# The second half's forget, query, gate and pool projections as 2x2x2 block products, in a streaming encoder trunk

## The chip, the core and the metric

The kernel runs on one core of a Trainium2 chip. The metric is the device time of one launch in microseconds (us). Six names are used below. PE is TensorE, the matrix engine, and its weight loads have a row of their own in the profile (PEld). DVE is VectorE, ACT is ScalarE, POOL is GpSimd, and SP is the engine whose queue issues nearly all transfers. Each engine runs its instructions in the order in which they stand in its own program, and waits on semaphores for the others.

## The reference, cut to what matters

One layer is applied to 2048 prompt tokens and to 32 tokens of a running stream (the sample). The width is 1024, everything is float32.

```
h = rmsnorm(x, g_pre_mix)
u, zq, zf, zi, zg = split(h @ w_in, ...)              # five times 512 columns
y_pool = window means of u (2, 4, 8, 16 frames) - u, then a 128x128 map per group
q = silu(zq);  fgate = lb + (1-lb)*sigmoid(zf);  kin = (1-lb)*sigmoid(-zf)
o, S1 = HGRN2 recurrence(q, kin, v = zi, log fgate)    # 4 heads of 128, state 128x128
y_hg = rmsnorm(o) * silu(zg)
x = x + rmsnorm(concat(y_pool, y_hg) @ w_out, g_post_mix)
h2 = rmsnorm(x, g_pre_ffn)
x = x + rmsnorm((silu(h2 @ w_gate) * (h2 @ w_up)) @ w_down, g_post_ffn)
```

The last 15 rows of u and the final states of the recurrence are outputs too, for the prompt and for the sample.

## The kernel before

**Precision.** A float32 operand is split into a high part, rounded by a cast on ACT, and a low part, the difference, made on DVE. A product of two such operands is three matmuls into one PSUM bank: high by high, high by low, low by high. All large products are matmuls of a 128x128 weight tile with 128x512 activations.

**Stages.** The prompt is cut in two halves of 1024 tokens, A and B, and the sample rides with B. A half runs through: values (the zi columns, lines of `values`), the front (16 column tiles of 128: forget, query and gate of four heads in `head_products`, then four tiles of u in `pool_products`), the projection by w_out (`project`), and gate and up (`gate_up`). The product by w_down is run for both halves at the end (`down`). In the trace the second half's values take 797 to 843 us, its front 843 to 1086 us, and its projection begins at 1086 us.

**Two ways of multiplying.** In the front a column tile is 8 row blocks of the weights by 2 blocks of 512 tokens by 3 matmuls, which is 48 matmuls into the banks `mmb`. In gate and up two column tiles of weights and the two blocks of tokens and of rows are taken as a 2x2x2 block product that needs seven block products where the plain way needs eight (a Strassen form). Its sums of activation blocks are made once per half (`first_forms`, `last_forms`), its sums of weight blocks for each pair of columns. A product is 12 matmuls into one of the banks `gx`, `gz`, `gy`, and four results `c11`, `c21`, `c22`, `c12` are put together from them by ACT (a copy of a bank) and DVE (an addition of a bank).

**What sets the order.** PE's order is written out: tasks (the recurrence of a head, the window sums, the loads of the next stage) are generators that are polled after every third matmul and that give the PE time until their next step. The other engines are ordered by the tile scheduler, which also gives out buffer slots. SP has one queue in order. Every matmul is recorded under the helper at line 202. Other lines that are spoken of: 1325 is the low part of a weight form in gate and up, 1427 the addition that empties the bank `gy` into `c22`, 1250 the low part of the hidden activations, 724 the copies of the values out of PSUM, 240 and 246 the low parts of weights, 858 a step of the recurrence on POOL (`k_t`), 929 its small copies (`attn`), and 1531 to 1547 the sums for the product by w_down, the only large two-input additions that POOL does here. `hst` and `hd` are the hidden activations on their way through DRAM, 256 KB a transfer.

## Time and profile before

| | |
|---|---|
| time, median of 3 runs | 2083.34 us (2080.56 to 2084.01) |
| span of the profiled execution | 2079.3 us |
| granted TensorE clock | 0.999 |
| PE busy | 2068.0 us, 99% of the span |
| DVE, ACT, POOL busy | 1418.5, 834.6 and 279.7 us |
| data moved | 319.49 MB |

The profiled execution has no time of its own beside its span; the median is 4.0 us longer than that span, and this difference is taken as what lies around a span. Busy times of PE are modelled, so its rate is read from stretches of the chain in which one kind of matmul follows another: a row "start, duration, what, xN" there gives the time per matmul.

### The profile page before, as it was taken

What the parts mean: (1) busy time and instruction counts of PE and PEld (TensorE: products, weight loads), DVE (VectorE), ACT (ScalarE), POOL (GpSimd) and SP (SyncE); (2) the same over time, 40 slices, a digit from 0 to 9 for tenths busy, and PEclk for the clock granted to TensorE, in tenths of its full rate; (3) what the DMA queues carried; (4) which work ended last, traced back from release to release, by engine and by line L of the source; (5) the groups of instructions that cost most, each with busy time, mean ns of one, the idle gap of its engine ahead of it and who ended that gap; (6) DMA issues with size and microseconds to landing.
All of it is one profiled execution on the core that took longest, in us unless ns stands there. A gap on an engine that the chain in (4) does not pass through costs nothing.

```text
span 2079.3 us, 34073 instructions
## 1 busy us (share of the span) xinstructions
PE 2068.0 (99%) x13093; PEld 1686.5 (81%) x13093; DVE 1418.5 (68%) x2288; ACT 834.6 (40%) x1656; POOL 279.7 (13%) x375
## 2 busy tenths in 40 slices
PE   9999999999999999999999999999999999999998
PEld 7788888888888888788888788888888778888876
DVE  5655665787777778465575697776666866566587
ACT  6444445654444445233334563444444521011032
POOL 0232302100000000122231200000000210110134
PEclk9999999999999999999999999999999999999999
DMA  8321144445555558211015614554445796776778
GB/s 288 115 88 42 44 142 162 132 127 167 161 153 152 157 172 260 70 46 36 26 54 177 200 52 137 163 149 139 147 137 173 231 335 203 218 226 200 219 223 220
DMA packets 391777, 319.49 MB, mean 154 GB/s; under 512 B 18216, under 2 KB 320800, under 8 KB 391616
## 3 DMA queue, kind: packets, MB, share of 16 engines
q1 hardware_dynamic: 389168, 309.41, 48.1%
q0 software_dynamic: 2016, 7.34, 1.9%
q8 instruction: 103, 1.69, 0.3%
q10 hardware_dynamic: 432, 0.57, 0.1%
q14 instruction: 58, 0.48, 0.1%
HBM read 216.79 MB, written 100.47 MB: 153 GB/s over the span
## 4 chain that ended last, share of the span: by engine, by line
PE 96%; DVE 2%; DMA 1%; ACT 0%; issue 0%; POOL 0%; DVEq 0%; SPq 0%; ACTq 0%; POOLq 0%
PE gx L202 23%; PE mmb L202 16%; PE gy L202 12%; PE dx L202 10%; PE ops L202 10%; PE gz L202 5%; PE dy L202 5%; PE vps L202 4%; PE dz L202 3%; PE gb L202 1%; PE gw L202 1%; PE gsps L202 1%; PE ups L202 1%; DVE acc L1605 1%; PE tps L345 1%; PE fps L202 1%
## 5 line engine op out<-in xcount | busy, mean ns | idle before, releaser
L202 PE MATMUL gx<-fhi,wf 128*128 128x512 f32 x1376 | 386.9, 391 | 0.0
L202 PEld LDWEIGHTS gx<-fhi,wf 128*128 128x128 f32 x1376 | 256.8, 188 | 54.9 <-issue 2.2
L202 PE MATMUL gx<-flo,wf 128*128 128x512 f32 x688 | 213.1, 390 | 0.0
L202 PE MATMUL gy<-fhi,wf 128*128 128x512 f32 x704 | 201.6, 390 | 0.0
L202 PE MATMUL dx<-dhi,hst 128*128 128x512 f32 x640 | 185.4, 391 | 0.8 <-DVE acc L1605 0.7
L202 PE MATMUL mmb<-hTlo,whi 128*128 128x512 f32 x512 | 175.3, 404 | 0.0
L202 PE MATMUL mmb<-hThi,whi 128*128 128x512 f32 x512 | 165.5, 404 | 0.0
L1605 DVE TENSOR_TENSOR acc<-dx,acc 128x512 f32<-128x512 f32 x168 | 115.1, 690 | 71.6 <-PE dx L202 70.6
L202 PE MATMUL mmb<-hThi,wlo 128*128 128x512 f32 x512 | 158.8, 391 | 0.0
L1325 DVE TENSOR_TENSOR wf<-s,wf 128x512 fp32r<-128x512 f32 x176 | 120.2, 690 | 56.0 <-ACT wf L1320 54.0
L202 PEld LDWEIGHTS gy<-fhi,wf 128*128 128x128 f32 x704 | 131.8, 188 | 28.1 <-DVE c L1427 0.4
L202 PEld LDWEIGHTS gx<-flo,wf 128*128 128x128 f32 x688 | 129.1, 188 | 27.0
L1320 ACT CAST wf<-s 128x512 fp32r<-128x512 f32 x176 | 108.1, 623 | 102.8 <-DVE s L1301 31.5
L202 PEld LDWEIGHTS dx<-dhi,hst 128*128 128x128 f32 x640 | 119.5, 188 | 30.1 <-issue 3.4
L1544 ACT CAST dhi<-t 128x1024 fp32r<-128x1024 f32 x20 | 20.7, 1055 | 249.8 <-DVE dlo L1545 181.6
L1325 DVE TENSOR_TENSOR wf<-wraw,wf 128x512 fp32r<-128x512 f32 x132 | 89.8, 687 | 34.4 <-ACT wf L1320 34.4
L202 PEld LDWEIGHTS mmb<-hTlo,whi 128*128 128x128 f32 x512 | 96.2, 188 | 20.5 <-issue 0.8
L202 PEld LDWEIGHTS mmb<-hThi,wlo 128*128 128x128 f32 x512 | 96.3, 188 | 18.9 <-issue 0.2
L1320 ACT CAST wf<-wraw 128x512 fp32r<-128x512 f32 x132 | 80.8, 622 | 75.8 <-PE gx L202 36.2
L202 PE MATMUL gy<-flo,wf 128*128 128x512 f32 x352 | 108.7, 389 | 0.0
L202 PEld LDWEIGHTS mmb<-hThi,whi 128*128 128x128 f32 x512 | 91.8, 188 | 20.6 <-issue 3.3
L202 PE MATMUL dx<-dlo,hst 128*128 128x512 f32 x320 | 98.6, 389 | 0.0
(326 smaller groups left out, 3974.8 us busy)
## 6 DMA issues: line engine op xcount, KB each, us to landing
hst<-hdFalse SPq DMA_DIRECT2D x140, 256.0 KB, 2.9
hst<-hdTrue SPq DMA_DIRECT2D x140, 256.0 KB, 3.0
wraw<-in_w_gate_dram SPq DMA_DIRECT2D x50, 512.0 KB, 4.0
wraw<-in_w_up_dram SPq DMA_DIRECT2D x50, 512.0 KB, 3.9
hdFalse<-hhi SPq DMA_DIRECT2D x77, 256.0 KB, 2.3
hdFalse<-hlo SPq DMA_DIRECT2D x77, 256.0 KB, 2.2
hdTrue<-hhi SPq DMA_DIRECT2D x77, 256.0 KB, 2.2
hdTrue<-hlo SPq DMA_DIRECT2D x77, 256.0 KB, 2.5
```

The source lines that it names most:

```text
L202: nc.tensor.matmul(out, l, r, start=start, stop=stop, skip_group_check=more)
L345: nc.tensor.transpose(ps[:, c:c + P], xn[:, (2 * kp + kk) * P:(2 * kp + kk + 1) * P], ident)
L1320: nc.scalar.copy(wf[:, 0], getattr(M, src) if isinstance(src, str) else src)
L1325: nc.vector.tensor_tensor(wf[:, 1], getattr(M, src) if isinstance(src, str) else src, wf[:, 0].bitcast(F32), ALU.subtract)
L1544: nc.scalar.copy(hi, src)
L1605: nc.vector.tensor_tensor(dst, ps, dst, ALU.add)
```

## The change

Only the second half's front is changed in what PE multiplies; the rest follows from it.

- **Products.** The 16 column tiles of half B are taken as 8 pairs (forget with query of a head, gate with gate of two heads, u with u of two groups). A pair is seven products of 12 matmuls, in the order 1, 2, 6, 7, 5, 4, 3, in `front_pairs`.
- **Weight forms.** They lie ready in DRAM (`wd`). Three of the seven are plain blocks, and half A's front writes their high and low parts out when it has them (`keep`, 48 writes of 256 KB). The other four are sums: a task in half A's gate and up (`weight_forms`) loads 32 blocks, makes 32 sums of 128x512 on POOL, 32 casts on ACT, 32 differences on DVE, and writes 64 tiles. Half B's front loads 112 tiles of 256 KB, three products ahead. From the second pair on, and within the first, each load stands behind a copy of one element on POOL, which reads a result tile of the product round and so marks the time from which the load may be issued.
- **Activation forms.** The normalised channels of half B are kept as four blocks. Three forms are plain blocks, which the values use too. The other four need two pairs of sums on DVE and two pairs on POOL (128x1024 each), 8 casts and 8 differences of 128x1024.
- **Space.** To hold the forms, values go to DRAM (`vd`) and come back for each head, the results of heads 0 to 2 go to `yd` and come back before the projection, the slots shrink to 1024 columns, and one pool of tiles grows from 21 to 25.
- **Sample.** Its loads and statistics move to the start of the program and its column tiles into half A's front, where the weights pass by anyway. Its recurrence is done for the four heads at once in a task of half B (`sample_mix`), instead of 32 extra columns in each head.
- **Recurrence and windows.** A head's recurrence is split in two tasks (its tail may run beside the next head), and the window sums take the frames before the half from small tiles. The projection of half B takes its row blocks in another order.

```diff
...
-NT = 21
+NT = 25
...
+FETCH = 3
+FORMS = 8000.0
 LOOKRAW = 2
-TMAX = HALF + NS
-SLOT = HALF + 64
+SLOT = HALF
...
-        KORDER = [4, 5, 2, 3, 0, 1, 6, 7]
+        KORDER = [[4, 5, 2, 3, 0, 1, 6, 7], [4, 5, 2, 3, 6, 7, 0, 1]]
+        COLS = (COL_F, COL_Q, COL_G, 0)
+        FQ, G, U = (lambda h: ((0, h), (1, h))), (lambda h: ((2, h), (2, h + 1))), (lambda g: ((3, g), (3, g - 1)))
+        PAIRS = [FQ(0), G(0), FQ(1), FQ(2), G(2), FQ(3), U(3), U(1)]
+        ROUND = (1, 2, 6, 7, 5, 4, 3)
+        wd = [DP.tile([7, P, 2, 512], F32, name=f"wd{i}") for i in range(len(PAIRS))]
+        vd = DP.tile([NH, P, NCH, P], F32, name="vd")
+        yd = DP.tile([NH - 1, 2, P, HALF], F32, name="yd")
...
+        def keep(w, kind, h):
+            n, m = pair_of(kind, h)
+            for p, kh in ((4, 1),) if m else ((1, 0), (2, 1)):
+                for i in range(2):
+                    nc.sync.dma_start(out=wd[n][p - 1, :, i, :], in_=w[1 + i][kh].bitcast(F32))
...
+        def weight_block(n, m, kh):
+            kind, h = PAIRS[n][m]
+            c0 = COLS[kind] + h * P
+            t = t2("wb", [P, 4, P])
+            nc.sync.dma_start(out=t, in_=w_in[kh * 512:kh * 512 + 512, c0:c0 + P].rearrange("(k p) c -> p k c", p=P))
+            return t.rearrange("p k c -> p (k c)")
...
+        def weight_forms():
+            def put(n, p, src):
+                hi, lo = t2("fhi", dt=F32R), t2("flo", dt=F32R)
+                nc.scalar.copy(hi, src)
+                nc.vector.tensor_tensor(lo, src, hi.bitcast(F32), ALU.subtract)
+                for i, t in enumerate((hi, lo)):
+                    nc.sync.dma_start(out=wd[n][p - 1, :, i, :], in_=t.bitcast(F32))
...
+            v = nc.gpsimd
+            for n in range(len(PAIRS)):
+                a21, a22 = weight_block(n, 1, 0), weight_block(n, 1, 1)
+                yield FORMS
+                v.tensor_tensor(a22, a21, a22, ALU.add)
+                a11 = weight_block(n, 0, 0)
+                yield FORMS
+                put(n, 5, a22)
+                v.tensor_tensor(a21, a11, a21, ALU.subtract)
+                v.tensor_tensor(a11, a22, a11, ALU.subtract)
+                a12 = weight_block(n, 0, 1)
+                yield FORMS
+                put(n, 7, a21)
+                v.tensor_tensor(a12, a12, a11, ALU.subtract)
+                yield FORMS
+                put(n, 6, a11)
+                yield FORMS
+                put(n, 3, a12)
...
+                    if tg == 0:
+                        nc.scalar.copy(hi[:, parts[i]], flat[:, parts[i]])
+                if tg:
+                    nc.scalar.copy(hi, flat)
+                for cs in parts:
+                    nc.vector.tensor_tensor(lo[:, cs], flat[:, cs], hi[:, cs].bitcast(F32), ALU.subtract)
...
+            b11, b21 = S.xT[0][0:2], S.xT[0][2:4]
+            b12, b22 = S.xT[1][0:2] if tg else None, S.xT[1][2:4] if tg else None
+            F = S.plain[tg]
+            if tg == 0:
+                S.F[1], S.F[2] = F[0:2], F[2:4]
+                return
+            S.F[3] = F[2:4]
+            v = nc.vector
+            yield 5000.0
+            sums(b12, b12, b11, ALU.subtract)
+            t2s = [ztile("t2s", [P, D]) for _ in range(2)]
+            sums(t2s, b22, b12, ALU.subtract)
+            yield 3000.0
+            S.F[6] = form(t2s)
+            sums(b11, t2s, b11, ALU.subtract, nc.gpsimd)
+            yield 3000.0
+            sums(b21, b21, t2s, ALU.subtract, nc.gpsimd)
+            S.F[7] = form(b11)
+            yield 3000.0
+            S.F[5] = form(b12)
+            yield 3000.0
+            S.F[4] = form(b21)
...
+            if not S.B:
+                for h in range(NH):
+                    for c in (COL_F, COL_Q, COL_G):
+                        want(lambda c=c, h=h: raw_cols(w_in, c + h * P))
+                for g in (3, 2, 1, 0):
+                    want(lambda g=g: raw_cols(w_in, g * P))
+                project_loads(S)
...
+                vt = t2("vt", [P, NH, P])
+                (nc.vector.tensor_copy if i % 2 else nc.scalar.copy)(vt, pss[i].rearrange("p (h c) -> p h c", c=P))
+                nc.sync.dma_start(out=vd[:, :, tg * 4 + i, :].rearrange("h p c -> p h c"), in_=vt)
...
+            def fetch(i, behind=None):
+                if i < len(seq):
+                    n, p = seq[i]
+                    wf[n, p] = [t2("wf", dt=F32R) for _ in range(2)]
+                    for j, t in enumerate(wf[n, p]):
+                        if behind is not None:
+                            nc.gpsimd.tensor_copy(t[0:1, 0:1], behind[0:1, 0:1])
+                        nc.sync.dma_start(out=t.bitcast(F32), in_=wd[n][p - 1, :, j, :])
+            def product(i, ps, start, behind):
+                n, p = seq[i]
+                fetch(i + FETCH, behind)
+                while p not in S.F:
+                    S.norm[1].step()
+                hi, lo = wf.pop((n, p))
+                for k in (0, 2):
+                    trios = [(hi[:, kk * P:(kk + 1) * P], lo[:, kk * P:(kk + 1) * P],
+                              *(x[:, (kk % 2) * 512:(kk % 2) * 512 + 512] for x in S.F[p][kk // 2])) for kk in (k, k + 1)]
+                    for m, (a, b) in enumerate(in_turn(trios)):
+                        mm(ps, a, b, start and k == 0 and m == 0, k == 2 and m == 5, rcost(512), not start)
+                        if m % 3 == 2:
+                            poll()
+            for i in range(FETCH):
...
+            c21 = None
+            add = ALU.add
+            for n, pair in enumerate(PAIRS):
+                i = n * len(ROUND)
+                for kh in pair:
+                    targets(S, *kh)
+                x = mmbank("gx")
+                product(i, x, True, c21)
+                c11 = t2("c11")
+                nc.scalar.copy(c11, x)
+                z = mmbank("gz")
+                product(i + 1, z, True, c21)
+                nc.vector.tensor_tensor(c11, z, c11, add)
+                use(S, *pair[0], c11, 0, 512)
+                product(i + 2, x, False, c11)
+                c21 = t2("c21")
+                nc.scalar.copy(c21, x)
+                y = mmbank("gy")
+                product(i + 3, y, True, c11)
+                c22 = t2("c22")
+                nc.scalar.copy(c22, y)
+                product(i + 4, x, False, c21)
+                nc.vector.tensor_tensor(c22, x, c22, add)
+                use(S, *pair[1], c22, 512, 1024)
+                if n + 1 == len(PAIRS):
+                    project_loads(S)
+                    ahead(Stream.used)
+                product(i + 5, y, False, c22)
+                nc.vector.tensor_tensor(c21, y, c21, add)
+                use(S, *pair[1], c21, 0, 512)
+                product(i + 6, x, False, c22)
+                use(S, *pair[0], x, 512, 1024)
+                if pair[0][0] == 0:
+                    S.hgrn = start_head(S, pair[0][1], 3500.0)
+                elif pair[0][0] == 3:
+                    for _, g in pair:
+                        S.pools[g] = S.pool = Task(pool_window(S, g, S.e[g]), 1500.0, after=S.pool)
+            S.hgrn.finish()
+            for h in range(NH - 1):
+                S.y[4 + h] = (ztile("yhi", dt=F32R), ztile("ylo", dt=F32R))
+                for i, t in enumerate(S.y[4 + h]):
+                    nc.sync.dma_start(out=t.bitcast(F32), in_=yd[h, i])
...
             yield 1200.0
+            if B:
+                S.tails = Task(hgrn_tail(S, H, h, spill, kds, vs, qa, t7), 0.0, after=S.tails)
+            else:
+                yield from hgrn_tail(S, H, h, spill, kds, vs, qa, t7)
...
+                while not hasattr(H, "g"):
+                    yield 2000.0
+                nc.vector.tensor_tensor(yr, yps, H.g[:, cols], ALU.mult)
+                if spill:
+                    for i, t in enumerate(two(yr)):
+                        nc.sync.dma_start(out=yd[h, i, :, cols], in_=t.bitcast(F32))
+                else:
+                    put_y(S, 4 + h, cols, yr)
...
+                    pairs = front_pairs(S)
+                    next(pairs)
...
+                if i:
+                    next(pairs, None)
+                else:
+                    for h in range(NH):
+                        head_products(S, h)
+                    for g in (3, 2, 1, 0):
+                        pool_products(S, g)
...
+                if i == 0:
+                    forms = Task(weight_forms(), 50000.0)
...```

The order of instructions shows the change at three places. First PE at the start of half B's front. Its rows before, where `hThi` and `hTlo` are the parts of the activations and `whi` and `wlo` those of the weights:

```order
L202 MATMUL vsps<-wrow,hsr 32x512 x4
L202 MATMUL mmb<-hThi_7402,whi 128x512
L202 MATMUL mmb<-hThi_7404,whi 128x512
L202 MATMUL mmb<-hTlo_7403,whi 128x512
L202 MATMUL mmb<-hTlo_7405,whi 128x512
L202 MATMUL mmb<-hThi_7402,wlo 128x512
L202 MATMUL mmb<-hThi_7404,wlo 128x512
```

and now, with `fhi`, `flo` the parts of an activation form and `wf` those of a weight form:

```order
L203 MATMUL vsps<-wrow,hsr 32x512 x4
L203 MATMUL gx<-fhi,wf 128x512 x2
L203 MATMUL gx<-flo,wf 128x512 x2
L203 MATMUL gx<-fhi,wf 128x512 x4
L203 MATMUL gx<-flo,wf 128x512 x2
L203 MATMUL gx<-fhi,wf 128x512 x2
L203 MATMUL gz<-fhi,wf 128x512 x2
L203 MATMUL gz<-flo,wf 128x512 x2
L203 MATMUL gz<-fhi,wf 128x512 x4
L203 MATMUL gz<-flo,wf 128x512 x2
L203 MATMUL gz<-fhi,wf 128x512 x2
L203 MATMUL gx<-fhi,wf 128x512 x2
```

A product is 12 matmuls, and the bank changes with it. In the whole program the matmuls on `mmb` go from 1536 to 768, and those on `gx`, `gz` and `gy` grow by 384, 96 and 192.

Second, DVE from the middle to the end of half B's values. Before, only low parts (`hlo` of half A's hidden activations, `wlo`) and sums for them stood between the last parts of the activations and the last copies out of the values' banks:

```order
L1250 TENSOR_TENSOR hlo<-c_7510,hhi 128x512
L246 TENSOR_TENSOR wlo<-wraw,whi 128x512 x2
L1250 TENSOR_TENSOR hlo<-hs,hhi 128x512
L1250 TENSOR_TENSOR hlo<-c_7360,hhi 128x512
L1243 TENSOR_TENSOR hs<-c_7360,hs 128x512
L724 COPY va<-vps 128x512
L724 COPY vb<-vps 128x512
```

Now (`xT` are the activation blocks, summed in place, `t2s` a sum, `flo` a form's low part, `vt` the values):

```order
L370 TENSOR_TENSOR xT<-xT 128x1024
L810 COPY vt<-vps 128x512
L370 TENSOR_TENSOR xT<-xT 128x1024
L370 TENSOR_TENSOR t2s<-xT 128x1024 x2
L365 TENSOR_TENSOR flo<-t2s,fhi 128x1024
L1500 TENSOR_TENSOR hs<-c_7884,c_8190 128x512
L365 TENSOR_TENSOR flo<-t2s,fhi 128x1024
L241 TENSOR_TENSOR wlw<-wrow,whw 128x1024
L1510 TENSOR_TENSOR hlo<-hs,hhi 128x512
L365 TENSOR_TENSOR flo<-xT,fhi 128x1024 x4
L1510 TENSOR_TENSOR hlo<-c_8087,hhi 128x512
L365 TENSOR_TENSOR flo<-xT,fhi 128x1024 x2
```

The four sums and eight differences of the forms now stand ahead of the last two copies of values that DVE does. POOL's four sums are released by the sums on `t2s`.

Third, POOL in the second and third pair, where a head's recurrence runs:

```order
L1018 TENSOR_TENSOR k_t<-k_t,tt 128x16x32
L920 CAST wf<-c_8956 1x1 x2
L1226 COPY attn_8818<-cmp 32x4x32 x4
L1226 COPY attn_8819<-cmp 32x4x32 x3
L1018 TENSOR_TENSOR k_t<-k_t,tt 128x8x64
L1226 COPY attn_8819<-cmp 32x4x32
L920 CAST wf<-c_9278 1x1 x4
L920 CAST wf<-c_9368 1x1 x2
```

The `CAST` rows are the markers, one for each of the two parts of a weight form. They are new on this engine, and stand among the steps of the recurrence that were there before.

599 lines of the change are left out of this document (337 added, 262 removed).

## The prediction

> **What bounds the kernel now.** I read the page first, for the engine that is full, then the windows of half B's front and of the stages around it, then the chain for the time of one matmul.
>
> ```profile
> span 2079.3 us, 34073 instructions
> PE 2068.0 (99%) x13093; PEld 1686.5 (81%) x13093; DVE 1418.5 (68%) x2288; ACT 834.6 (40%) x1656; POOL 279.7 (13%) x375
> PE 96%; DVE 2%; DMA 1%; ACT 0%; issue 0%; POOL 0%; DVEq 0%; SPq 0%; ACTq 0%; POOLq 0%
> L202 PE MATMUL mmb<-hTlo,whi 128*128 128x512 f32 x512 | 175.3, 404 | 0.0
> hst<-hdFalse SPq DMA_DIRECT2D x140, 256.0 KB, 2.9
> ```
>
> PE is 99% of the span and 96% of the chain. No idle time stands before the matmuls of the front (last column 0.0), so a matmul taken out of it shortens the chain by its own time, as long as nothing else takes its place.
>
> Columns of the windows: length, then busy us (instructions) of PE, PEld, DVE, ACT, POOL, the granted clock, the DMA share, GB/s.
>
> ```profile
> 450.00:800.00 350.00, 350.00 (x1545) 289.64 (x1544) 263.22 (x416) 163.20 (x287) 3.38 (x7) 1.00 0.56 166
> 842.00:1086.00 244.00, 244.00 (x2846) 198.72 (x2839) 148.18 (x329) 81.86 (x236) 67.00 (x93) 1.00 0.15 44
> 1620.00:2000.00 380.00, 379.82 (x1704) 304.24 (x1703) 238.47 (x322) 63.70 (x90) 49.58 (x21) 1.00 0.76 233
> ```
>
> The second row is the front that changes: PE 244.00 of 244, DVE 61%, ACT 34%, POOL 27%, DMA 0.15. There is room on every other engine. The first row is half A's gate and up, where the weight forms are to be made: DVE is at 263 of 350 there, POOL all but free.
>
> The group means (404 ns) are the latency of a pipelined matmul. The rate is in the chain:
>
> ```profile
> 791.65 5.44 PE gx L202 x24
> 797.09 32.64 PE vps L202 x144
> 841.83 0.99 PE vsps L202 x8
> 842.83 7.71 PE mmb L202 x33
> 902.74 1.85 PE ups L202 x16
> ```
>
> 32.64 us for 144 and 5.44 for 24 are both 226.7 ns per 128x512 matmul, whichever bank it writes. The front begins at 842.83; I call the corresponding moment T0.
>
> **The change, term by term, against the span of 2079.3 us.**
>
> *Matmuls.* Removed: 768 x 0.2267 = 174.1 us. Added: 56 products x 12 = 672 x 0.2267 = 152.3 us (2.72 us a product). Net −21.8 us. Accumulating into a bank round by round doesn't change the rate: the `gx` row above is such a product.
>
> *Sample.* Its column tiles move from one full stage of PE into another: nothing. Batching its recurrence removes 12 fp32 matmuls of 128x128, two records each, at 0.116 us a record (1.85 / 16): −2.8 us. It adds five of that kind (+1.2) and one four times as wide (4 x 0.23, +0.9), and drops three transposes of one record each (−0.3). Net −1.0; bounds −2 and 0.
>
> *First pair, activation forms.* DVE before, around the end of the values:
>
> ```profile
> 802.12 1.41 DVE L493 SCALAR_TENSOR_TENSOR xT<-xT,cons,rb 128x512 f32<-128x512 f32 x2 [4.17 <-DMA rb<-roots]
> 822.40 1.23 DVE L240 TENSOR_TENSOR wlw<-wrow,whw 128x1024 fp32r<-128x1024 f32 x1
> 823.54 0.69 DVE L1250 TENSOR_TENSOR hlo<-hs,hhi 128x512 fp32r<-128x512 f32 x1
> 828.45 0.69 DVE L1243 TENSOR_TENSOR hs<-c,hs 128x512 f32<-128x512 f32 x1
> 839.15 0.69 DVE L724 COPY va<-vps 128x512 f32<-128x512 f32 x1 [10.01 <-PE vps L202]
> ```
>
> DVE is solid from 802.12 to 829.14 and then has 10.01 us free. A 128x1024 operation takes 1.14 us of its queue (822.40 to 823.54), a 128x512 one 0.6. After the change DVE has between the same points 8 scalings (5.6 us by the first row), 12 differences, 5 weight parts and 4 sums of 128x1024 (21 x 1.14 = 23.9), and 7 operations of 0.6 (4.2): 33.7 us, to 835.8. What makes this dearer is POOL, which makes four of the sums in that time. How the two engines get on stands at the end of gate and up, the one place where POOL does such sums now:
>
> ```profile
> 1609.38 0.69 DVE L1240 TENSOR_TENSOR hs<-c,c 128x512 f32<-128x512 f32 x1
> 1611.31 1.62 POOL L1532 TENSOR_TENSOR t<-wdr,t 128x512 f32<-128x512 f32 x1
> 1611.70 1.78 DVE L1545 TENSOR_TENSOR dhl<-wdr,dhl 128x512 fp32r<-128x512 f32 x1
> 1612.89 1.74 POOL L1533 TENSOR_TENSOR t<-wdr 128x512 f32<-128x512 f32 x1
> 1613.62 1.56 DVE L1545 TENSOR_TENSOR dhl<-t,dhl 128x512 fp32r<-128x512 f32 x1
> L1531 POOL TENSOR_TENSOR t<-wdr 128x1024 f32<-128x1024 f32 x5 | 12.0, 2400 | 108.6 <-DMA wdr<-in_w_down_dram 82.3 <-DVE acc L1605 17.8 <-PE gx L202 8.5
> ```
>
> A DVE operation that takes 0.69 us alone took 1.78 and 1.56, and ended 0.55 us after the POOL sum that ran beside it; so while POOL sums, DVE does one operation per sum. Four sums of 2.4 us are 9.6 us in which DVE does 4 x 1.14: 5.0 us lost, to 840.8. The copy of values that PE's second product needs stands behind all of it and must be done by T0 + 2.7 = 845.5. Cover of about 4 us; without it, up to 5 us if sums and casts serialise.
>
> [...]
>
> *First pair, weights.* The loads of the fourth product stand in SP's queue behind the last four writes of values, which wait for copies after the values' last matmul. An issue takes 0.49 us and a load lands 2.9 us later:
>
> ```profile
> 1655.59 3.42 SPq L1558 DMA_DIRECT2D hst<-hdTrue  x7
> ```
>
> Copies to T0 + 1.5, six issues (2.9), landing (2.9): T0 + 7.3, needed at T0 + 8.2. Both parts of the first pair together: 0 to 6, and I take 2, nearer the covered end, since both sums come out in time but by 1 to 4 us.
>
> *Later pairs.* A load is issued three products ahead, 8.2 us. Behind its marker stand: the drain of the bank on DVE (0.69), the copy on POOL, the issues (1.0 for two), the landing (2.9): 4.9 us with an idle POOL (0.33 for the copy, an eighth of the row of copies below), so 3.3 us to spare. Bandwidth is no limit: 512 KB per 2.72 us is 193 GB/s at most, and 233 GB/s were moved in the third window beside PE at 379.82 of 380. But the markers stand in POOL's queue behind a head's recurrence:
>
> ```profile
> 952.98 1.50 POOL L858 TENSOR_TENSOR k_t<-k_t,tt 128x512 f32<-128x512 f32 x1 [2.25 <-issue]
> 954.50 2.62 POOL L929 COPY attn<-cmp 32x128 f32<-32x128 f32 x8
> ```
>
> A step and the eight copies are 4.1 us, 0.8 more than there is to spare, once per head: 3 us if a marker meets it each time. Behind a marker that waits stand the recurrence's next steps on POOL, and PE's small matmuls that use them are late in turn. The same steps hold DVE, as above. Bounds 0 and 10 (four heads, two such meetings of 1.2 us each); I take 2.
>
> *Transfers without a price.* The 48 writes of half A's front, the values' way through DRAM and the reloads of `yd` fall into stages where the DMA share is 0.15 to 0.56; if one is late, it is a wait of one landing, 2.9 us, at one place, and lies within the bounds above.
>
> *Gate and up of half A.* 32 sums on POOL, 32 differences on DVE (22 us of the 87 that are free there), 32 casts on ACT; the traffic grows by 25 MB in some 320 us, 166 to 245 GB/s, near what the third window carried. PE feels DVE at one place per 19 us round, where `gy` is emptied:
>
> ```profile
> 506.71 0.69 DVE L1427 TENSOR_TENSOR c<-gy,c 128x512 f32<-128x512 f32 x1
> 508.61 0.62 PE L202 MATMUL gy<-fhi,wf 128*128 128x512 f32 x2
> ```
>
> The bank is free at 507.40 and written again at 508.61: 1.2 us to spare. A sum of 128x512 on POOL (1.62) holds a DVE operation up by 1.1, just inside; the two sums that stand together hold two, and are outside by 1.0. Eight such groups: 0 to 8, and I take 1, since a group meets the drain in few of the 19 us.
>
> *Start of the projection.* The last pair is u, and its window sums end on DVE. After the last product DVE has, in its order, 18 operations of 0.6, 7 of 1.14 to 1.2 and three small ones: 19 us to the last low part. PE reads it after some 76 matmuls, 17.2 us. And the first weight part stands behind the last head's output, late by 0.6. I take 2.5; bounds 1 (reads partly covered by the order of row blocks) and 5 (as above with POOL's share).
>
> The sum: 2079.3 − 21.8 − 1.0 + 2 + 2 + 1 + 2.5 = 2064.0 for the span, 15.3 us less. The median of the runs is 4.0 above the span, so 2068 us.
>
> **Rivals.**
>
> *All of it stays* (the covers hold everywhere): 2083.3 − 21.8 − 1.0 = 2060.5. For it: the covers above are there on paper. Against it: two of them are under 1.5 us.
>
> *The weight stream is late in every round.* Before, nothing of the front's weights waited for a result; now each fetch runs through DVE, POOL and SP. It decides when drain, marker and landing exceed 8.2 us, that is a landing over 6.2 or a POOL queue over 3.3 us. 0.3 us on each of 56 products is 17 us and leaves 2083.3 − 22.8 + 17 + 5.5 = 2083; 0.7 us makes 2105. For it: SP's queue is in order and holds writes that wait. Against it: landing is 2.9 at 233 GB/s.
>
> *POOL's sums hold DVE, and DVE holds PE in gate and up*, on the other side: eight rounds have a single sum, a pair and a single sum. If each meets a drain with DVE's queue full, a single costs 1.62 − 1.2 = 0.4 and a pair 3.2 − 1.2 = 2.0, 2.8 a group, 22 in all: 2083.3 − 22.8 + 22 + 6.5 = 2089, slower. It decides from 2 us a group on. For it: the 1.78 us above. Against it: the groups are spread over 320 us and forms of weights can wait. [...]
>
> *It doesn't do what it says*: the order of instructions has the 96 matmuls less, so only a slower rate would do it, about 2083.
>
> **How the numbers follow.** Chances: the sum, with 2062 to 2076 as its own range, 0.66; all stays 0.10; weights late 0.12 (0.06 of it faster, 0.03 within, 0.03 slower); POOL and DVE 0.10 (0.01, 0.01, 0.08); no effect 0.02. The predicted time is 2068. The range runs from 2059 (sample at its better bound) to 2085 (every product a little over 0.3 us late). What this measurement tells from no change is about 0.2%, 4.2 us. Faster by more: 0.66 + 0.10 + 0.06 + 0.01 = 0.83; within: 0.03 + 0.01 + 0.02 = 0.06; slower: 0.03 + 0.08 = 0.11.
>
> **What would show it.** The stretch from the values' last matmul to the projection's first should be about 244 − 22 = 222 us, with PE idle of 1 to 4 us in its first 12 us and in the first 20 of the projection. Idle before `gx`, `gy`, `gz` put down to a transfer of `wf` is the late stream; idle before `gy` put down to DVE between 450 and 800 us is the third rival. If gate and up of half A is longer than before by over 3 us, my price there is wrong; if the front is shorter by less than 15 us, that of the later pairs is.

## The result and the profile after

The change is not faster but a little slower: 2088.32 us, median of 5 runs (2085.35 to 2091.79), against 2081.29 us for the kernel before in 5 runs beside it (2080.56 to 2084.01). The ratio is 1.0029, with a 95% interval of 1.0017 to 1.0041. The prediction was 2068. The profiled execution of the kernel after is the fastest of its five (2085.35 us), so its stages below come to some 3 us less than the median; where those 3 us lie no trace shows. Time and span of one execution lie 1.7 to 1.9 us apart in all runs, not the 4.0 taken ahead of the prediction, so the forecast span of 2064.0 stands for 2066 rather than 2068, which changes nothing in what follows.

The page of the kernel after, its head, the totals of the engines and the shares of the chain of waits:

```profile
span 2083.6 us, 34762 instructions
PE 2054.5 (99%) x12980; PEld 1667.7 (80%) x12980; DVE 1476.4 (71%) x2320; ACT 850.1 (41%) x1663; POOL 378.9 (18%) x544
PE 82%; DVE 9%; DMA 3%; issue 2%; ACT 2%; POOL 1%; SPq 0%; DVEq 0%; ACTq 0%; POOLq 0%
```

PE did less: 12980 records against 13093, and 13.5 us less busy time. But the span is 4.3 us longer, and PE's share of the chain fell from 96% to 82%: other engines, DVE first, now set the end in places.

The stages, from the first matmul of each on PE to the first of the next (in the last stage to PE's end), in us, from one profiled execution of each version. The last three columns are versions that are told of below: weight sums on DVE, activation sums on DVE, and the last version.

| stage | before | after | weight sums on DVE | activation sums on DVE | last version |
|---|---|---|---|---|---|
| front A | 233.8 | 254.5 | 254.7 | 253.0 | 249.5 |
| projection A | 90.7 | 91.0 | 91.0 | 91.0 | 91.0 |
| gate and up A | 422.7 | 429.9 | 423.6 | 430.2 | 424.5 |
| values B | 45.8 | 47.0 | 46.2 | 45.8 | 45.8 |
| front B | 243.7 | 215.9 | 215.7 | 212.5 | 209.5 |
| projection B | 97.5 | 100.0 | 102.1 | 99.1 | 101.1 |
| gate and up B | 452.4 | 453.6 | 453.2 | 453.4 | 453.3 |
| down | 434.9 | 434.5 | 434.3 | 434.5 | 434.8 |

Where the time went is read from this table first. By the prediction's terms the products and the batched recurrence save 22.8 us in front B. The sample's column tiles leave front B for front A. Their matmuls take 11.1 us, start to start, in either kernel. Before the change they stand in 32 bursts; 22 of these hold other small matmuls too, so that PE returns from small to 512-wide matmuls there in any case. For the other 10 the returns add some 1.4 us: in the trace of before the 512-wide matmul behind such a burst takes 0.31 or 0.34 us to the next start, where one in a row takes 0.227, and the one before a burst of 16 takes 0.32. So the tiles are worth about 12.5 us in each place, an estimate from the two traces. Front B should have fallen by about 35 us and front A risen by 12.5. Front B fell by 27.8, front A rose by 20.7, and gate and up of A, in which PE's work is unchanged, rose by 7.2. Losses of some 27 us ate a gain of 22.8: front A 8, gate and up of A 7, values 1, front B 7.5, projection B 2.5, gate and up of B 1.

What PE waited for, from the groups of waits of the kernel after (total us, times, longest):

```profile
PE gy L203 <- DVE c L1687: 6.1, 6, 1.4
PE kps L1238 <- POOL k_t L1018: 2.4, 1, 2.4
PE ops L203 <- DVE on L1061: 2.4, 1, 2.4
PE ops L203 <- DVE wlo L247: 1.2, 1, 1.2
PE gx L203 <- DMA wf<-wd: 0.9, 1, 0.9
PE vps L203 <- DVE wlw L241: 0.9, 1, 0.9
PE gz L203 <- DVE vt L810: 0.7, 1, 0.7
PE gy L203 <- DMA wf<-wd: 0.5, 1, 0.5
```

Line 203 is the old 202, and 1687 the old 1427. The weight stream hardly appears: 1.4 us in two waits. What appears is DVE and POOL. The windows of gate and up of A and of the inner part of front B after (columns as in the prediction):

```profile
450.00:800.00 350.00, 346.48 (x1524) 285.44 (x1523) 298.49 (x438) 171.66 (x309) 50.35 (x36) 1.00 0.74 223
860.00:1079.00 219.00, 213.04 (x2447) 170.05 (x2447) 143.75 (x285) 80.03 (x202) 101.19 (x213) 1.00 0.55 178
```

In the first, PE went from 350.00 to 346.48 busy and did 21 matmuls fewer in the same 350 us, while DVE rose by 35 us for 22 operations more.

### The profile page after: what moved, and what is told of

The parts are those of the page before. It is cut to its first block, busy times and chain, and to the rows that moved or that the text cites. A ratio compares the mean times of both kernels' runs of the same rounds, so it can differ in the third digit from the quotient of the medians.

```text
span 2083.6 us, 34762 instructions
## 1 busy us (share of the span) xinstructions
PE 2054.5 (99%) x12980; PEld 1667.7 (80%) x12980; DVE 1476.4 (71%) x2320; ACT 850.1 (41%) x1663; POOL 378.9 (18%) x544
## 4 chain that ended last, share of the span: by engine, by line
PE 82%; DVE 9%; DMA 3%; issue 2%; ACT 2%; POOL 1%; SPq 0%; DVEq 0%; ACTq 0%; POOLq 0%
PE gx L203 23%; PE gy L203 12%; PE dx L203 10%; PE ops L203 9%; PE mmb L203 7%; PE gz L203 5%; PE dy L203 5%; PE dz L203 3%; PE vps L203 1%; PE gb L203 1%; PE gw L203 1%; PE gsps L203 1%; DMA xt<-in_x_prompt_dram 1%; DVE acc L1865 1%; DVE wf L1585 1%
## 5 line engine op out<-in xcount | busy, mean ns | idle before, releaser
L203 PE MATMUL gx<-fhi,wf 128*128 128x512 f32 x1632 | 462.7, 392 | 0.9 <-DMA wf<-wd 0.9
L203 PEld LDWEIGHTS gx<-fhi,wf 128*128 128x128 f32 x1632 | 303.8, 188 | 67.0 <-issue 3.5
L203 PE MATMUL gx<-flo,wf 128*128 128x512 f32 x816 | 256.7, 392 | 0.0
L203 PE MATMUL gy<-fhi,wf 128*128 128x512 f32 x832 | 241.1, 392 | 6.6 <-DVE c L1687 6.1
L203 PEld LDWEIGHTS gy<-fhi,wf 128*128 128x128 f32 x832 | 154.7, 188 | 41.3 <-DVE c L1687 7.2
L203 PE MATMUL dx<-dhi,hst 128*128 128x512 f32 x640 | 185.3, 391 | 0.8 <-DVE acc L1865 0.7
L203 PEld LDWEIGHTS gx<-flo,wf 128*128 128x128 f32 x816 | 153.2, 188 | 32.0
L1585 DVE TENSOR_TENSOR wf<-s,wf 128x512 fp32r<-128x512 f32 x176 | 126.0, 723 | 43.6 <-ACT wf L1580 42.3
L1580 ACT CAST wf<-s 128x512 fp32r<-128x512 f32 x176 | 108.0, 621 | 115.2 <-PE gy L203 26.8
L203 PEld LDWEIGHTS dx<-dhi,hst 128*128 128x128 f32 x640 | 119.6, 188 | 30.0 <-issue 3.4
L203 PE MATMUL gy<-flo,wf 128*128 128x512 f32 x416 | 131.2, 392 | 0.0
L203 PE MATMUL gz<-fhi,wf 128*128 128x512 f32 x384 | 112.2, 393 | 0.7 <-DVE vt L810 0.7
L1580 ACT CAST wf<-wraw 128x512 fp32r<-128x512 f32 x132 | 80.6, 621 | 77.9 <-PE gx L203 37.4
L1585 DVE TENSOR_TENSOR wf<-wraw,wf 128x512 fp32r<-128x512 f32 x132 | 92.7, 711 | 23.3 <-ACT wf L1580 23.2
L203 PE MATMUL dx<-dlo,hst 128*128 128x512 f32 x320 | 98.6, 389 | 0.0
L203 PE MATMUL dy<-dhi,hst 128*128 128x512 f32 x320 | 98.5, 389 | 0.0
L203 PEld LDWEIGHTS gy<-flo,wf 128*128 128x128 f32 x416 | 78.1, 188 | 16.3
L203 PE MATMUL mmb<-hTlo,whi 128*128 128x512 f32 x256 | 90.8, 411 | 0.2
L1865 DVE TENSOR_TENSOR acc<-dy,acc 128x512 f32<-128x512 f32 x88 | 60.6, 689 | 38.4 <-PE dy L203 38.0
```

Source lines behind the costliest of these rows:

```text
L203: nc.tensor.matmul(out, l, r, start=start, stop=stop, skip_group_check=more)
L1580: nc.scalar.copy(wf[:, 0], getattr(M, src) if isinstance(src, str) else src)
L1585: nc.vector.tensor_tensor(wf[:, 1], getattr(M, src) if isinstance(src, str) else src, wf[:, 0].bitcast(F32), ALU.subtract)
L1865: nc.vector.tensor_tensor(dst, ps, dst, ALU.add)
```

## Gate and up of A: the wait in the trace

One round of the kernel after, from the timeline of POOL, of DVE, and of PE (start, duration, operation, in brackets the idle time before):

```profile
502.34 1.29 POOL L474 TENSOR_TENSOR wb<-wb 128x512 f32<-128x512 f32 x1 [2.59 <-ACT wf L1580]
503.71 1.61 POOL L475 TENSOR_TENSOR wb<-wb 128x512 f32<-128x512 f32 x1
...
501.55 0.69 DVE L1510 TENSOR_TENSOR hlo<-c,hhi 128x512 fp32r<-128x512 f32 x1
502.37 1.80 DVE L1585 TENSOR_TENSOR wf<-s,wf 128x512 fp32r<-128x512 f32 x1
504.10 1.77 DVE L1585 TENSOR_TENSOR wf<-wraw,wf 128x512 fp32r<-128x512 f32 x1
505.80 0.68 DVE L1692 TENSOR_TENSOR c<-gy,c 128x512 f32<-128x512 f32 x1
...
510.83 0.68 DVE L1510 TENSOR_TENSOR hlo<-hs,hhi 128x512 fp32r<-128x512 f32 x1
511.43 0.68 DVE L1687 TENSOR_TENSOR c<-gy,c 128x512 f32<-128x512 f32 x1
...
512.26 0.70 PE L203 MATMUL gy<-fhi,wf 128*128 128x512 f32 x2 [1.39 <-DVE c L1687]
```

Two POOL sums hold two DVE operations of 0.69 us to 1.80 and 1.77. That is 2.2 us, as the prediction had it. But DVE has next to no idle time from there to 511.43, so the 2.2 us are still in its queue 7 us later, when the drain of `gy` comes up. PE waits 1.39 us. The sums need not fall on the drain; they need only fall anywhere since DVE last was idle. Three of the stage's five waits for `gy`, 3.2 of 4.9 us, are of this kind. The last of them (1.37 us, at 813.6) is not: the last sum is 25 us back and DVE was idle for 3.0 and 2.4 us in between. It takes 0.9 to 1.7 us in every version with the sums on POOL and up to 1.0 in those without, and how it comes about is not shown.

## Experiments on the weight forms

**Sums on DVE.** The 32 sums of weight blocks stay, on the other engine:

```diff
-            v = nc.gpsimd
+            v = nc.vector
```

> The 32 sums of weight blocks in half A's gate and up are made on DVE instead of POOL; nothing else changes. If it is POOL's sums that hold DVE (a DVE operation of 0.69 us took 1.77 beside them), the stage from the projection's end to the values, 430.0 us after the change and 422.7 before it, should come to 423 to 426 us and the total to about 2083, although DVE gets 32 x 0.6 = 19 us more of its own work. If DVE is simply too full there, the stage grows: 432 us or more, total 2090 or more.

Measured: 2080.34 us in 10 runs (2077.55 to 2082.94), against 2082.36 for before beside it, ratio 0.9992 (0.9982 to 1.0001). That is no difference from before, and 8 us less than the change. Gate and up of A falls from 429.9 to 423.6, as the theory had it.

**No sums.** The plain blocks are split and stored where the sums would be:

```diff
-                v.tensor_tensor(a22, a21, a22, ALU.add)
-                v.tensor_tensor(a21, a11, a21, ALU.subtract)
-                v.tensor_tensor(a11, a22, a11, ALU.subtract)
-                v.tensor_tensor(a12, a12, a11, ALU.subtract)
```

> The 32 sums of weight blocks are left out, so that plain blocks are split, written and used in place of the sums; the loads, casts, differences and writes stay, and the order of PE's products too. This leaves out a part of the computation. If POOL's sums are the cause in gate and up, the stage returns to 423 to 425 us and the total falls by 5 to 7, to 2081 to 2083. If the 32 differences on DVE and the traffic are the cause, the stage stays at 428 to 430 and the total at 2088.

Measured: 2081.96 us, ratio 0.9998 (0.9989 to 1.0008); gate and up of A 423.3.

**No forms.** The task of the weight forms is gone, and the second half loads stored plain blocks in place of forms 3, 5, 6 and 7:

```diff
-            forms.finish()
-                if i == 0:
-                    forms = Task(weight_forms(), 50000.0)
-  ... in_=wd[n][p - 1, :, j, :])
+  ... in_=wd[n][{5: 1, 7: 2, 6: 4, 3: 1}.get(p, p) - 1, :, j, :])
```

> The whole task that makes the weight forms is left out (32 loads, sums, casts, differences, 64 writes); the second half loads the plain forms in place of the sums, as many transfers as before. This leaves out a part of the computation. Whatever of the task delays PE, the stage is then 422.7 us as before the change, and the total 2081. If the 7.3 us come from something else (the start of half B's front, which now has more to do at the end of this stage), it stays above 426 us. With e1 and e2 it splits the loss between POOL's sums and the rest of the task.

Measured: 2081.54 us, ratio 0.9993 (0.9983 to 1.0002); gate and up of A 422.9, against 422.7 before.

So the casts, differences, loads and writes of the forms cost 0.4 us together (422.9 against 423.3), the sums themselves 0.3 on DVE, and the same sums on POOL 6.6. These are figures of one profiled execution each. The other versions put the stage at 427.8, 430.2 and 432.5 us with the sums on POOL and at 423.7 to 424.6 with them on DVE, so the loss by POOL is beyond doubt and its size known to some 2 us. The window 450 to 800 us of the three, in the order sums on DVE, no sums, no forms:

```profile
450.00:800.00 350.00, 350.00 (x1546) 289.70 (x1545) 294.17 (x475) 175.88 (x316) 3.09 (x4) 1.00 0.75 228
```

```profile
450.00:800.00 350.00, 350.00 (x1545) 289.62 (x1544) 276.63 (x444) 175.87 (x317) 2.81 (x4) 1.00 0.75 228
```

```profile
450.00:800.00 350.00, 350.00 (x1545) 289.64 (x1544) 261.29 (x415) 160.58 (x286) 3.38 (x4) 1.00 0.54 158
```

PE is at 350.00 in all three. The fifth figure is DVE. Without sums it is busy for 276.63 us. With the sums on DVE itself it is 294.17, 17.5 more; with the sums on POOL it was 298.49, 21.9 more, for six operations fewer in the window (438 against 444). Handing the sums to POOL did not relieve DVE: it cost DVE more time than making them would have, and in larger lumps. A pair puts 1.2 us of DVE's own work into its queue when it is made there (two times 0.6) and 2.2 us of hold when POOL makes it, and the slack before the drain was 1.2. PE's waits for `gy` on DVE in this stage fell from 4.9 us in five to 0.4 in one.

The gain of the whole change is still missing in all three, though: with gate and up put right, the time is that of before. The other losses have to be in the fronts.

## Experiments on the fronts

**The sample's column tiles.** Front A's rise is told apart by leaving the tiles out:

```diff
+            nc.gpsimd.memset(Smp.z, 0.0)
-            if S.B:
+            if True:
                 return
```

> The sample's column tiles are left out of half A's front (its projections are zero then), everything else as in the change. This leaves out a part of the computation. Half A's front was 233.8 us without them before the change and 254.5 with them after it. Matmuls of them: 11.2 us, and 21 returns to the large matmuls at 0.23: 4.9. If these 16 are all, and the other 4.6 are a wait of the recurrence for POOL and the low clock behind it, the front comes to 238 here, and the wait of 2.4 us for k_t stays. If the sample's tiles shift the recurrence so that it waits, the wait goes and the front is 234.

Measured: 2074.75 us in one run; front A 238.7, so the tiles and what hangs on them are 15.8 us of its rise of 20.7. Neither expectation came whole: the stage is near the first one's 238, but the wait for `k_t` is gone, as the second had it. In the kernel after this wait and the low clock behind it (told at the end) come to about 4 us (2.4 and 1.5); in so far as both went, they are in the 15.8. A return is some 0.14 us in the trace of before (1.4 for 10), where the expectation had 0.23. Of the 4.9 us of excess that remain without the tiles, 1 is a wait for a recurrence state, and some 3 lie at the start of the stage. The kernel after loses time there too. The windows before and after:

```profile
60.00:65.00 5.00, 5.00 (x24) 4.14 (x23) 5.00 (x10) 4.32 (x10) 0.53 (x1) 1.00 0.00 0
```

```profile
60.00:65.00 5.00, 4.66 (x18) 2.95 (x17) 5.00 (x9) 4.93 (x10) 0.00 (x0) 1.00 1.05 355
```

PE does 18 matmuls where it did 24. The last high parts of the activations come later from ACT (its last cast of them ends at 66.6 us, before the change at 63.9), and PE goes on in short stops, only part of which are idle time. DMA traffic is new in this window; whether it is the reason was not tested.

**The recurrence in front A.** The longest wait of the kernel after in that stage, from the timelines of POOL, DVE and PE:

```profile
258.29 4.53 POOL L1226 COPY attn<-cmp 32x128 f32<-32x128 f32 x4 [0.29 <-PE lv L203]
262.91 1.97 POOL L1018 TENSOR_TENSOR k_t<-k_t,tt 128x512 f32<-128x512 f32 x1
...
260.16 1.20 DVE L1326 TENSOR_TENSOR sa<-sb 128x1017 f32<-128x1017 f32 x1
261.48 1.20 DVE L1326 TENSOR_TENSOR sb<-sa 128x1009 f32<-128x1009 f32 x1
...
264.93 1.09 PE L1238 MATMUL kps<-cons,k_t 128*128 128x128 f32 x8 [2.40 <-POOL k_t L1018]
```

Four small copies on POOL take 4.53 us beside DVE's window sums. One such copy takes 0.28 to 0.30 us in most places; here they take 1.20, 0.66, 1.28 and 1.27, and each ends some 0.15 us after the DVE operation beside it, while the sums keep their 1.20. Behind them stands the step that makes `k_t`, and PE waits 2.40 us for it. The same wait, of 2.39 or 2.40, stands in the versions with no sums, with no forms and with sums on DVE: it has nothing to do with the weight forms. It goes with the sample's tiles, as seen above. Before the change these copies met the window sums too (three of them took 3.26 us from 243.88 on), and PE did not wait; that the tiles shift the last head's recurrence on PE against the sums fits this, but was not tested by itself. The edit takes the copies off POOL, in both halves:

```diff
-                    nc.gpsimd.tensor_copy(attn[sb][...], cmp_[sb][...])
+                    nc.scalar.copy(attn[sb][...], cmp_[sb][...])
```

> The small copies into the attention tiles (8 per head, both halves) are made on ACT instead of POOL. In half A's front four of them took 4.53 us on POOL beside DVE's window sums, and PE then waited 2.4 us for the step of the recurrence behind them, after which the clock was granted at 0.66 for 5 us. If that is the loss there, half A's front (49.2 to 394.7, 345.5 us) falls by 3 to 4 us, PE's wait for k_t goes, and the total falls to 2084. If PE waits for something else behind it, the wait moves and the total stays within 1 us of 2088.

Measured: 2086.21 us (2082.22 to 2091.91), ratio 1.0019 (1.0010 to 1.0029). Front A is 3.6 us shorter and the wait for `k_t` is gone, both as expected. Front B is 2.0 us longer: there ACT became late for PE.

```profile
PE ups L203 <- ACT kd L1241: 1.4, 1, 1.4
```

The copies belong on ACT in half A and on POOL in half B.

**The four activation sums on DVE.** The prediction gave the first pair of front B 2 us, with four sums of 128x1024 on POOL. Timeline of DVE and of POOL in the kernel after:

```profile
852.55 3.31 DVE L365 TENSOR_TENSOR flo<-t2s,fhi 128x1024 fp32r<-128x1024 f32 x1
855.77 2.87 DVE L1500 TENSOR_TENSOR hs<-c,c 128x512 f32<-128x512 f32 x1
858.56 3.42 DVE L365 TENSOR_TENSOR flo<-t2s,fhi 128x1024 fp32r<-128x1024 f32 x1
861.91 3.42 DVE L241 TENSOR_TENSOR wlw<-wrow,whw 128x1024 fp32r<-128x1024 f32 x1
...
851.60 3.16 POOL L370 TENSOR_TENSOR xT<-t2s,xT 128x1024 f32<-128x1024 f32 x1 [63.34 <-PE vps L203]
854.72 3.37 POOL L370 TENSOR_TENSOR xT<-xT,t2s 128x1024 f32<-128x1024 f32 x1
858.05 2.85 POOL L370 TENSOR_TENSOR xT<-t2s,xT 128x1024 f32<-128x1024 f32 x1
860.86 3.38 POOL L370 TENSOR_TENSOR xT<-xT,t2s 128x1024 f32<-128x1024 f32 x1
```

Both engines are drawn out. The DVE operations, 1.22 or 0.69 us alone, take 2.87 to 3.42, and the sums, 2.40 alone, 2.85 to 3.38. The starts alternate, one operation here and one there. From 852.55 to 865.33 DVE got through work of 4.3 us in 12.8: 8.4 us lost, where the prediction had 5.0 from its row. The POOL sums take longer beside DVE's operations too, by 0.45 to 0.98 us each. Strictly in turn, four sums of 2.40 and this work of 4.3 would take 13.9 us; from the first sum's start to the last operation's end they took 13.7.

```diff
-            sums(b11, t2s, b11, ALU.subtract, nc.gpsimd)
+            sums(b11, t2s, b11, ALU.subtract)
-            sums(b21, b21, t2s, ALU.subtract, nc.gpsimd)
+            sums(b21, b21, t2s, ALU.subtract)
```

> The change with one edit: the four activation-form sums of the second half (four sums of 128x1024 on POOL, 1.6 to 1.7 us each by 512 elements when beside DVE) on DVE instead; the 32 weight-form sums stay on POOL. Theory (the two engines take turns at their shared access in both directions, so a sum costs DVE more from POOL than on DVE itself): in the change, DVE operations beside these sums took 2.9 to 3.4 us against 0.7 to 1.2 alone, and the first pair's PE waits were 2.1 us (0.7, 0.5, 0.9); with the sums on DVE at 1.22 us each the waits in the first 15 us of the second front fall to under 1 us, and values plus front are about 1 to 2 us shorter than the change's 262.9. Rival (the four sums are off the path and the waits come from the weights' landing): waits and stage within 0.5 us of the change. Gate and up of the first half stays at about 430, since the 32 sums there are untouched; if it falls, that loss was not theirs.

Measured: 2078.5 us in one run. Values B 45.8, as before the change, and front B 212.5: 4.6 us less in the two. No wait of PE is left between 813 and 948 us. DVE in the same stretch of this version, with four of the sums now among its own operations:

```profile
852.63 2.34 DVE L365 TENSOR_TENSOR flo<-t2s,fhi 128x1024 fp32r<-128x1024 f32 x2
854.89 1.21 DVE L370 TENSOR_TENSOR xT<-t2s,xT 128x1024 f32<-128x1024 f32 x1
856.03 1.21 DVE L241 TENSOR_TENSOR wlw<-wrow,whw 128x1024 fp32r<-128x1024 f32 x1
```

The low part of the values' last weights is done at 857.24 where it was done at 865.33. Gate and up of A stayed at 430.2: its loss belongs to the other 32 sums. The waits named in the expectation gave 2.1 us and the removal 4.6. Matmul for matmul, the two traces differ by these 4.6 us between 865 and 891 us and nowhere else in the two stages: the waits of 2.1, the 0.9 us wait in values, and about 1.6 us that are not idle time of PE, some 0.3 us in the first two matmuls behind each of these four waits and as much at two more places. The loads of `wf` are three products ahead as before, so the two waits for them came of DVE's delay in the main; one of 0.4 us is back in the next version.

## Towards a better version

**The three together.** Both kinds of sums on DVE, the copies of half A alone on ACT, and a longer planned pause between a head's two output groups in half B:

```diff
-                    nc.gpsimd.tensor_copy(attn[sb][...], cmp_[sb][...])
+                    (nc.gpsimd.tensor_copy if S.B else nc.scalar.copy)(attn[sb][...], cmp_[sb][...])
-                yield 800.0 if S.B and sb == 0 else 4500.0
+                yield 3500.0 if S.B and sb == 0 else 4500.0
```

> Four waits taken away together: the weight forms' 32 sums on DVE (e1), the attention copies of half A on ACT (e4, half B's stay on POOL), the four sums of activation forms on DVE instead of POOL, and the second output product of a head's tail 3.5 instead of 0.8 us after the first in the order of PE, so that it doesn't wait for its bank. If the two engines' shared access is what costs, the 128x1024 differences at the end of the values, 3.3 to 3.4 us beside POOL, take 1.2, the wait of gz for the copy of values (0.7) goes, and half A's front gives back 3.6 (as in e4). With e1's 8, e4's 3, 1 for the forms and 2.4 for the bank: 2074. If the losses aren't additive because the next wait stands close behind, 2077 to 2080.

Measured: 2075.25 us (2073.13 to 2076.71), ratio 0.9962 (0.9949 to 0.9974). Gate and up of A is 423.7, values 45.8, front A 252.3 with no wait for `k_t`. The pause did nothing: the wait of 2.4 us for `on` stood as before.

**Projection loads earlier.** The loads and first splits of the projection weights are put before the fifth product of the last pair, where they stood before the sixth, and the split reaches one weight further (the expectations call this two products earlier):

```diff
+                if n + 1 == len(PAIRS):
+                    project_loads(S)
+                    ahead(Stream.used + 1)
                 product(i + 4, x, False, c21)
-                if n + 1 == len(PAIRS):
-                    project_loads(S)
-                    ahead(Stream.used)
                 product(i + 5, y, False, c22)
```

> As c1, and the loads and the first weight part of half B's projection are issued two products earlier. The waits of the projection's first matmuls (0.6 for ACT's high part, 1.2 for DVE's low part) should go if the weights are simply split too late: 1.5 to 2 us less than c1. If the slots for them come free only with the last products, nothing changes, or weight loads of the last pair come late and it is slower.

Measured: 2078.99 us, ratio 0.9985 (0.9976 to 0.9994), slower than without it. The projection is 3.2 us shorter (97.8 against 101.0), front B 5.8 longer. ACT's timeline in this version shows why:

```profile
1062.00 0.59 ACT L960 COPY c<-gy 128x512 f32<-128x512 f32 x1
1068.15 1.14 ACT L246 CAST whi<-wrow 128x512 fp32r<-128x512 f32 x2 [5.57 <-DMA wrow<-in_w_out_dram]
1069.19 1.06 ACT L1241 COPY kd<-kps 128x512 f32<-128x512 f32 x2
```

The cast stands in ACT's queue ahead of the copy `kd` and waits 5.57 us for its load. PE waits 6.2 us for `kd`.

**One product more of lead.** The weights of the front are fetched four products ahead:

```diff
-FETCH = 3
+FETCH = 4
```

> As c1, with weight forms loaded four products ahead instead of three. The waits for a transfer of wf (0.5 and 0.9 us in the first pair, after the change) go: 1 to 1.5 us less than c1 if only the first pair's loads are late, and more if fetches are late in later rounds in a way that the waits don't name. If slots are short, it is the same or slower.

Measured: 2073.83 us (2073.09 to 2075.34), ratio 0.9958 (0.9942 to 0.9973). Front B 214.3 against 215.9, and no wait of PE for `wf` in it. The totals of this and of the version without it overlap, and in that version the clock was 0.66 over the five microseconds behind the 2.4 us wait for `on` (985 to 990 us) and here 1.00 (see the end), a loss of some 1.7 us, as much as the two fronts differ by. So the gain of the lead alone is not settled.

**A gap that is a gap.** The wait for `on` in that version, from the timelines of ACT, POOL, DVE and PE:

```profile
980.90 0.76 PE L203 MATMUL gb<-f_t,k_t 128*32 128x32 f32 x64
...
981.69 0.20 ACT L1057 ACTIVATION_READ_ACCUMULATOR junk<-ops 128x1 f32 x1
981.97 0.19 POOL L1058 TENSOR_SCALAR ost<-ost 128x4 f32<-128x4 f32 x1 [6.99 <-ACT junk L1057]
982.25 1.01 POOL L1059 TENSOR_TENSOR ost<-ost,nhalf 128x4 f32<-128x4 f32 x1
...
983.29 0.69 DVE L1061 TENSOR_TENSOR on<-ops,ost 128x512 f32<-128x512 f32 x1 [1.53 <-POOL ost L1059]
984.04 0.49 PE L203 MATMUL ops<-vh,attn 128*128 128x128 f32 x2 [2.37 <-DVE on L1061]
```

The second output group needs the bank of the first, which is free when its normalization is done, a chain of four squares on ACT, two small steps on POOL and one on DVE, which ends at 983.98, 3.7 us after the group's last matmul (980.28). Between the two stand three 512-wide matmuls and a burst of 64 small ones, which took 0.76 us. The planned pause is made of planned matmul times, and the burst's plan was far longer than its time.

```diff
-                yield 3500.0 if S.B and sb == 0 else 4500.0
+                yield 9000.0 if S.B and sb == 0 else 4500.0
```

> The faster variant (2073.8 us: weight-form and activation-form sums on DVE, attention copies of the first half on ACT, fetches four products ahead) with one edit: after the first of a head's two output groups in the second half, the plan waits 9000 instead of 3500 planned ns before it issues the second. In the program's order some 14 matmuls of 128x512 or more now stand between the two, 3 us and more of work, where before there were three and a burst of small ones. Theory (the 2.4 us wait of PE before the second group is that group waiting for the bank or the normalization of the first, a chain ACT 1.9, POOL 1.2, DVE 0.7 us): the wait goes, front of the second half 214.3 to about 212, total about 2071.5. Rival (the chain's end moves with it, or the last head then ends later and the projection waits instead): front shorter, projection longer by as much, total within 1 us of 2073.8.

Measured: 2071.81 us (2070.41 to 2072.84), ratio 0.9951 (0.9935 to 0.9968). The wait is gone. Front B falls by 4.8 us to 209.5, and the projection rises by 3.4 to 102.9, since the last head's tail ends later: both theories had their part. The ratio overlaps that of the version without the pause, which moreover was granted a mean clock of 0.998 in all four of its runs, where this one had 0.999 in all four, so the gain of the pause is not settled either.

**The split of the first projection weights.** With one edit more:

```diff
+                if n + 1 == len(PAIRS):
+                    ahead(Stream.used + 1)
                 product(i + 6, x, False, c22)
```

> The same with one more edit: the second half's first two projection weights are split into high and low parts one product before the front's last matmul, behind the last head's state matmuls on ACT, instead of at the first use. In the variant before, ACT begins that split at 1075.81, behind the last head's eight squares, though the load was issued at 1065.2; PE waits 1.35 and 0.68 us for it. Theory (the start of the projection waits for the place of the split in ACT's queue, not for the load): both waits fall under 0.3, projection 99.5 to about 97.5, total 1.5 to 2 us under the kernel beside it. Rival (ACT then waits for the load and holds the last head's copies, as with the loads two products earlier, where PE waited 6.2 us for kd): a new wait of PE before the last head's outputs of 2 us or more and no gain.

Measured: 2070.41 us (2069.57 to 2072.36) against 2082.0 for before in 7 runs, ratio 0.9945 (0.9930 to 0.9960). Against the version without it the runs overlap. The two waits at which the edit aimed were already down to 0.40 and 0.19 us there and are 0.40 and 0.22 here, so neither theory of this run is borne out. No new wait for the last head came up either.

This last version is the best of all: 11.6 us under before, and 17 to 18 under the change. Beside the change it has the 32 weight sums and the four activation sums on DVE, half A's `attn` copies on ACT, fetches four products ahead, a longer pause between output groups, and an earlier split.

## Why the prediction was wrong, point by point

- **Matmuls (−21.8) and sample (−1.0).** Borne out as far as it can be read. Front B should come to 243.7 − 22.8 − 12.5 = 208.4 us once nothing else is in the way. The last two versions reach 209.5, of which 2.0 and 2.1 us are idle PE. The tiles' move at "nothing" holds for the tiles themselves (about 12.5 us in either front).
- **Gate and up of A (+1).** This is the step that failed first: measured 7.2, of which the POOL sums are 6.6, where 1 was allowed. The price of one sum was right (1.1 us of hold, a pair 2.2). The condition was wrong: "a group meets the drain in few of the 19 us" takes the delay for one that passes with the sum. DVE, busy for 298 of 350 us, carried it for 7 us to the next drain. Room on DVE was not what lacked: with the sums on DVE it was busy for 294 of the 350 us and PE lost nothing in that window.
- **The rival "POOL's sums hold DVE"** named the place (`gy` emptied into `c22`), the way there (POOL holds DVE, and DVE holds PE) and the side of the result. It had 2.8 us a group, 22 in all; the measured cost is 6.6. Its chance of 0.10 was too low, and its "against" (groups are spread, forms can wait) is not what decides.
- **First pair (+2, bounds 0 to 6).** The waits in front B were 0.7, 0.5 and 0.9 us, 2.1 in all. By the experiment the whole term is 4.6, values included, and lies within the bounds. The sums were held to cost DVE 5.0 us with POOL unhindered; it was 8.4, with both engines held.
- **Weights late in every round** did not happen. The waits on `wf` were two, 1.4 us in all, in the first pair; they were gone with the activation sums on DVE, at three products of lead.
- **Later pairs (+2, bounds 0 to 10).** The one large wait, 2.4 us, was not a marker behind a recurrence on POOL but a bank of the recurrence's split tail, which the prediction did not name.
- **Front A (no term of its own).** The second step that failed: "from one full stage of PE into another: nothing" prices matmuls and not what they push. The stage lost 8 us beyond the tiles' own time, no less than gate and up of A. About 4 are the wait of 2.4 us for `k_t`, with POOL's copies held as above, and the lower clock behind it (below); some 2 are the late high parts at its start; the rest is smaller waits and was not taken apart. The activations and the recurrence of half A, whose timing changed with the sample's work and the new transfers, had no term.
- **Start of the projection (+2.5).** Measured 100.0 against 97.5, so 2.5 as forecast; the waits at its start in the trace (0.6, 1.2 and 0.9 us, for ACT's high parts and DVE's low part) add up to 2.7. Whether they came of the 19 us of DVE's work was not tested.
- **Values B and gate and up of B** had no term and cost 1.2 each; the first is the same hold by the activation sums, where the second comes from is open.

The terms allowed 7.5 us of losses and there were some 27. The prediction's own tests said so beforehand: gate and up of A longer by over 3 us, and idle before `gy` put down to DVE between 450 and 800 us. The front was 215.9 us where 222 was forecast; that looked like success and was not, because the forecast forgot that the tiles' 12.5 us leave it.

## What to carry to other kernels

The sums that were handed from a busy DVE to an idle POOL were not free for DVE here: they cost it 0.68 us a sum on POOL against 0.55 on DVE itself. The 2.2 us that a pair put into DVE's queue were still there 7 us later, as DVE had hardly been idle, so compare such a delay, up to where the queue is next idle, with the slack of every consumer and not only of the one beside it. When work moves between two full stages, price the neighbours that it shifts against each other, and check a planned gap against measured durations.

## What the runs showed of the hardware

**Taking turns.** In the first pair of front B DVE and POOL operations held each other up in both directions: DVE 1.22 to 3.3 or 3.4 us, POOL 2.40 to between 2.85 and 3.38 (128x1024). What the two share there the traces do not show. Small copies on POOL with one input, 0.28 to 0.30 us each in most places, took up to 1.28 beside DVE's window sums of 1.20 in front A (258.29 to 262.83 us), which were not held.

**Clock after a stall.** The granted clock fell behind some waits of PE. The kernel after and the version with activation sums on DVE run the same work up to there and have the same wait at the same time (262.53 to 264.93 and to 264.92). Their windows behind it (the figure behind POOL's is the clock):

```profile
265.00:270.00 5.00, 5.00 (x37) 4.17 (x38) 1.71 (x4) 2.02 (x3) 0.37 (x3) 0.66 0.34 105
```

```profile
265.00:270.00 5.00, 5.00 (x47) 4.37 (x48) 2.68 (x7) 2.02 (x3) 0.37 (x3) 1.00 0.35 105
```

The clock is 0.66 in one and 1.00 in the other, for 37 and 47 matmuls; front A is 1.5 us shorter in the second, so about 1.5 of that version's gain is this. In steps of half a microsecond the clock of the kernel after is 1.00 up to 266.0, 0.51 and then 0.50 from there to 269.0, 0.57 up to 269.5 and 1.00 from there on: some 3.4 us at half rate (266.0 to 269.4), an estimate from these steps, and (3.4 × 0.5 + 1.6) / 5 is the 0.66 of the row. Of eleven waits of 2.4 us in eight versions, five for `k_t` and six for `on`, five had 0.66 over five microseconds from about their end: those for `k_t` in the kernel after and in the versions with sums on DVE, with no sums and with no forms, and that for `on` in the version with the three together. The other six had 1.00. Behind a wait of 1.92 us in the version with activation sums on DVE (up to 684.25 us) the rate did not fall: 44 matmuls of 128x512 took the 9.98 us from 684.82 on, 0.227 us each. After the 6.2 us wait of the version with early loads the five microseconds from 1070 on were granted 0.50.

```profile
1070.00:1075.00 5.00, 5.00 (x20) 4.71 (x21) 3.81 (x9) 0.26 (x1) 0.00 (x0) 0.50 1.03 422
```

Why the same wait was followed by the lower clock in one version and not in another is not shown. In the kernel after such a wait of 2.4 us cost PE some 1.5 us more than itself.
